# Prompt attention scores in two float32r passes with stacked query parts, and attention begun beside the third head

## The chip, the cores and the metric

The kernel runs on one core of one Trainium2 chip, in one launch. The metric is the device time of a launch in microseconds (us); smaller is better.

## The reference, cut to what matters

One layer of a hybrid decoder: a normalised input of 1024 prompt tokens and 64 sample tokens (8 sequences of 8) goes through one input projection whose columns feed a pooling mixer (256), a gated linear recurrence (HGRN2, 4 heads, 512) and a cross-attention (4 heads of 64) into 256 memory tokens. Their outputs are joined to 1024 columns and go through an output projection, then a gated feed-forward block. The change concerns the cross-attention of the prompt:

```python
def cross_attn(qx, mem_k, mem_v):
    q = qx.reshape(B, L, XATTN_HEADS, XATTN_DH).astype(jnp.float32)
    s = jnp.einsum("blhd,bmhd->bhlm", q, mem_k.astype(jnp.float32)) * (XATTN_DH ** -0.5)
    p = jax.nn.softmax(s, axis=-1)
    o = jnp.einsum("bhlm,bmhd->blhd", p, mem_v.astype(jnp.float32))
```

## The kernel before, in words

Everything lies feature by token: a tile has 128 features on the partitions and tokens along the free axis. Projections are done in float32r: each operand is split into a high part (a copy rounded to float32r, on ACT) and a low part (the rest, by a subtraction on DVE), and a product takes three matmuls, high by high, high by low and low by high (`gemm`, L282 to L284). One projection is 8 slices of the input times 3 token chunks of 362 or 364 columns.

The projections follow a list of six windows (`WIN`, L228). Letters name the columns: `q`, `i`, `f` a head's query, value and forget gate, `x` the attention's queries (two tiles `qx`, two heads of 64 features each), `g` the output gates, `u` the pooling input. Beside each window run generators: `hgrn(h)` the recurrence of a head, `xattn()` the attention, `pool_mix()` the pooling. `weave` calls the projections one after the other and takes from each generator as many steps (yields) as it is given a count for; `drain` runs a generator to its end. The order in which each engine gets its instructions follows from this, from due waits between tiles and from the free buffers, in a scheduler that sorts by priority.

In `xattn()` first the sample tokens are done: scores against the cached keys, a softmax, transposes, and eight blocks of value products into the tile `so` (L614; each block 32 small matmuls of 16 columns). Then follows the prompt, in eight blocks of 128 tokens. `scores(n)` makes four matmuls in float32, one per head: 64 features (one half of the partitions) by 128 queries and 256 memory keys (L631, into `xs`). A softmax follows on DVE and ACT. The next step transposes the probabilities on PE (`xtp`, L647), copies them on ACT (`xt`, L648), multiplies them with the memory values (`xo`, L655, 32 matmuls of 32 output columns each) and copies the result into `cat` on ACT (L658). Scores run one block ahead.

After the last window comes the output projection (`po`, L953 to L955). It needs the eight tiles of `cat` in high and low parts (`c`, L915 and the line after it) and its weights split (`ow000h`, L924, and `ow000l`, L925).

Other names in the rows: `pu` and `pg` are the projections of `u` and `g`, `oss` (L809) the sums of a head's squares, `Us` (L822) the state product of the sample tokens with 64 rows, `pp` (L555) the pooling mixer's matmul, `kv` (L478, L481) the memory projection, `whi` and `wlo` (L213, L214) the parts of the weights.

Of the kernel before, what the change touches and what calls it, by code (L numbers as in the profile page):

```python
# [10 lines left out]
F32 = mybir.dt.float32  # L11
F32R = mybir.dt.float32r
I32 = mybir.dt.int32
U8 = mybir.dt.uint8
AF = mybir.ActivationFunctionType
ALU = mybir.AluOpType
# [4 lines left out]
NP = 1024  # L21
# [6 lines left out]
RB = 34  # L28
# [22 lines left out]
def trunk(ctx, tc, I, O):  # L51
    nc = tc.nc
    const = ctx.enter_context(tc.tile_pool(name="const", bufs=1))
    rowp = ctx.enter_context(tc.tile_pool(name="rowp", bufs=1))
# [18 lines left out]
    mm = nc.tensor.matmul  # L73
    act = nc.scalar.activation
    tt = nc.vector.tensor_tensor
# [3 lines left out]
    def row(name, cols=1106, p=128):  # L79
        return rowp.tile([p, cols], F32, tag="row", name=name, bufs=RB)  # L80

    def hrow(name, cols=512, p=128, dt=F32):
        return now["wk"].tile([p, cols], dt, tag="half", name=name, bufs=HB)
# [10 lines left out]
    def bank(name, shape):  # L94
        if now["name"] == "down":
            return acc(name, shape)
        return now["psB"].tile(shape, F32, tag="b", name=name)
# [44 lines left out]
    for k in range(KT):  # L142
# [3 lines left out]
        if k % 2 == 0:  # L146
            q = slice(k * 128, k * 128 + 256)
# [71 lines left out]
    def weights(i, ahead=1):  # L219
# [8 lines left out]
    WIN = [  # L228
        [("q", 1), ("i", 1), ("f", 2)],
        [("q", 2), ("i", 2), ("f", 3)],  # L230
        [("q", 3), ("i", 3), ("x", 0), ("x", 1)],
        [("g", 0), ("g", 1)],
        [("u", 0), ("u", 1)],
        [("g", 2), ("g", 3)],
    ]
# [256 lines left out]
    mkT, mvt = memkv()  # L492
# [67 lines left out]
    def softmax(name, ps, p):  # L560
        mx, sm = tiny(f"{name}mx", 2), tiny(f"{name}sm", 2)
        nc.vector.tensor_reduce(out=mx, in_=ps, axis=AX.X, op=ALU.max)
        ts(out=mx, in0=mx, scalar1=-0.125, scalar2=None, op0=ALU.mult)
        for j in range(2):
            act(out=p[:, j, :], in_=ps[:, j, :], func=AF.Exp, bias=mx[:, j:j + 1], scale=0.125, accum_out=sm[:, j:j + 1])
        nc.vector.reciprocal(out=sm, in_=sm)
        for j in range(2):
            ts(out=p[:, j, :], in0=p[:, j, :], scalar1=sm[:, j:j + 1], scalar2=None, op0=ALU.mult)
# [6 lines left out]
    def xattn():  # L575
        qs = hrow("qs").rearrange("p (f b c) -> p f b c", f=2, b=8)
        nc.gpsimd.memset(qs, 0.0)
        for ft in range(2):
            cat[6 + ft] = row(f"cat{6 + ft}", NT)
            for half in range(2):  # L580
                P = slice(64 * half, 64 * half + 64)
                h = 2 * ft + half
                nc.gpsimd.tensor_copy(out=qs[P, ft, :, h * 8:h * 8 + 8],
                                      in_=qx[ft][P, NP:NT].rearrange("p (b l) -> p b l", b=8))
        ssc = bank("ssc", [128, 2, 256])
        svt = []
        for b in range(0, 8, 2):
            kts = [hrow(f"skt{b + i}").rearrange("p (f m) -> p f m", f=2) for i in range(2)]
            for i in range(2):
                nc.sync.dma_start(out=kts[i], in_=I["skT"][b + i])  # L590
            for ft in range(2):
                for i in range(2):
                    o = 32 * ((b + i) % 4)
                    mm(ssc[o:o + 32, b // 4, :], qs[:, ft, b + i, :], kts[i][:, ft, :], start=ft == 0, stop=ft == 1,
                       tile_position=(0, o))
            yield
        spr = hrow("spr").rearrange("p (g m) -> p g m", g=2)
        softmax("xs", ssc, spr)
        yield
        stp = bank("stp", [128, 4, 128])  # L600
        for i in range(4):
            nc.tensor.transpose(stp[:, i, :], spr[:, i // 2, (i % 2) * 128:(i % 2) * 128 + 128], ident)
        spT = hrow("spT").rearrange("p (g t c) -> p g t c", g=2, t=2)
        act(out=spT, in_=stp.rearrange("p (g t) c -> p g t c", g=2), func=AF.Copy)
        yield
        so = bank("so", [128, 2, 8, 16])
        for b in range(8):
            v_ = hrow(f"svt{b}").rearrange("p (t f) -> p t f", t=2)
            nc.sync.dma_start(out=v_, in_=I["sv"][b])
            for ft in range(2):  # L610
                for t in range(2):
                    o = 32 * (b % 4) + 16 * ft
                    for c in range(0, 128, 32):
                        mm(so[c:c + 32, ft, b, :], v_[:, t, ft * 128 + c:ft * 128 + c + 32], spT[:, b // 4, t, o:o + 16],  # L614
                           start=t == 0, stop=t == 1, tile_position=(0, c))
            yield
        for ft in range(2):
            for half in range(2):
                P = slice(64 * half, 64 * half + 64)
                act(out=cat[6 + ft][P, NP:NT].rearrange("p (b l) -> p b l", b=8),  # L620
                    in_=so[P, ft, :, half * 8:half * 8 + 8], func=AF.Copy)
        yield
        probs = {}

        def scores(n):
            pr = [hrow(f"xp{n}{hf}").rearrange("p (f m) -> p f m", f=2) for hf in range(2)]
            scs = [bank(f"xs{n}{hf}", [128, 2, 256]) for hf in range(2)]
            for ft in range(2):
                for hf in range(2):
                    P = slice(64 * hf, 64 * hf + 64)  # L630
                    mm(scs[hf][:, ft, :], qx[ft][P, n * 128:n * 128 + 128], mkT[P, ft, :], start=True, stop=True)  # L631
            for hf in range(2):
                softmax(f"x{n}{hf}", scs[hf], pr[hf])
            probs[n] = pr

        scores(0)
        for n in range(8):
            if n < 7:
                scores(n + 1)
            yield  # L640
            pr = probs.pop(n)
            ps = bank(f"xo{n}", [128, 2, 128])
            pT = [hrow(f"xt{n}{hf}").rearrange("p (f t l) -> p f t l", f=2, t=2) for hf in range(2)]
            for hf in range(2):
                tp = bank(f"xtp{n}{hf}", [128, 4, 128])
                for i in range(4):
                    nc.tensor.transpose(tp[:, i, :], pr[hf][:, i // 2, (i % 2) * 128:(i % 2) * 128 + 128], ident)  # L647
                act(out=pT[hf], in_=tp.rearrange("p (f t) l -> p f t l", f=2), func=AF.Copy)  # L648
            for ft in range(2):
                for t in range(2):  # L650
                    for hf in range(2):
                        h = 2 * ft + hf
                        for c in range(0, 64, 32):
                            o = 64 * hf + c
                            mm(ps[o:o + 32, ft, :], mvt[:, t, h * 64 + c:h * 64 + c + 32], pT[hf][:, ft, t, :],  # L655
                               start=t == 0, stop=t == 1, tile_position=(0, o))
            for ft in range(2):
                act(out=cat[6 + ft][:, n * 128:n * 128 + 128], in_=ps[:, ft, :], func=AF.Copy)  # L658
            yield
# [180 lines left out]
    def weave(units, *fillers, finish=1.0):  # L840

        done = [0] * len(fillers)
        for i, u in enumerate(units):
            for t, _ in enumerate(u()):
                part = min(1.0, (4 * i + t + 1) / (finish * 4 * len(units)))
                more = True
                while more:
                    more = False
                    for j, (g, n) in enumerate(fillers):
                        if done[j] < int(part * n + 1e-6):  # L850
                            next(g, None)
                            done[j] += 1
                            more = True
# [4 lines left out]
    def units(lst, chunk_major=False):  # L858
        if chunk_major:
            o = [(nm, j, c) for c in range(3) for nm, j in lst]  # L860
        else:
            o = [(nm, j, c) for nm, j in lst for c in range(3)]
        return [lambda nm=nm, j=j, c=c: project(nm, j, c, EV[nm](j)) for nm, j, c in o]

    hg = [hgrn(h) for h in range(4)]
    HS, XS, PS = 20, 31, 9
# [7 lines left out]
    drain(hg[1])  # L874
    head_rows(3)
    qx = [row(f"qx{j}", NT) for j in range(2)]
    weave(units(WIN[2]), (hg[2], HS))
    drain(hg[2])
    xa, pm = xattn(), pool_mix()
    weave(units(WIN[3]), (hg[3], HS), (xa, 16))  # L880
    drain(hg[3])
    nc.gpsimd.dma_start(out=O["pstate"], in_=sout)
    up, us, sbs = pool_rows()
    weave(units(WIN[4]), (xa, 10))
    weave(units(WIN[5], True), (pm, PS), (xa, 5), finish=0.7)
    drain(pm, xa)


# [709 lines left out]
    for mi in range(2):  # L1598
        for i in (0, 2):
            x = X[mi, 1, 0][:, i:i + 2]  # L1600
# [117 lines left out]
```

## Time and profile before

| what | us |
|---|---|
| median of 3 runs | 1228.74 (1227.69 to 1230.68) |
| the profiled execution | 1228.64 |
| its span | 1226.9 |

The span is the time from the first to the last instruction that the profiler shows. In a timeline each row is a run of instructions of one line: its start, the time from its first start to its last end, the line, the operation, the result and the operands, the form (rows by columns of the array that a matmul uses, then partitions by columns of the data) and how many records. Ends of matmuls are modelled and overlap; the distance from start to start tells the pace. A matmul in float32 has two records, one in float32r has one, but both are shown as f32. Stages of the program begin at about 188 us (third window, projections of `x` at 224), 259 (fourth), 312 (fifth), 351 (sixth) and 402 (output projection).

### The profile page before, as it was taken

How to read it: one execution, taken by the hardware profiler on the slowest of the kernel's cores; microseconds unless marked ns; L12 is line 12 of the kernel's file. 1: busy time of each engine (PE TensorE's matmuls, PEld its weight loads, DVE VectorE, ACT ScalarE, POOL GpSimd, SP SyncE). 2: the span in 40 equal slices, each digit the busy share in tenths (PEclk: the TensorE clock that was granted, in tenths of full speed). 3: DMA queues.
4: the chain of work that ended last, by engine and by line, in shares of the span. 5: the costliest groups of instructions: out<-in, count | busy, mean ns of one | idle time of the engine just before them, and what ended most of it. 6: DMA issues, size and time to landing. Idle time of an engine off the chain costs nothing.

```text
span 1226.9 us, 27524 instructions
## 1 busy us (share of the span) xinstructions
PE 1192.4 (97%) x11332; PEld 1148.2 (94%) x11332; DVE 925.3 (75%) x1675; ACT 545.4 (44%) x1044; POOL 260.9 (21%) x297
## 2 busy tenths in 40 slices
PE   6999999999999999899999999999999999999996
PEld 6999898978878899899999999999999999999996
DVE  7685869487877458989779878987786969868534
ACT  7743534223455455743333332333333445554542
POOL 0000000000000001445454554544323000100242
PEclk9999999999999999999999999999999999999998
DMA  8031111223102643213454354344212597345333
GB/s 270 27 121 53 37 53 53 78 79 120 39 23 91 236 135 115 89 61 132 146 191 139 107 173 159 119 157 158 89 53 70 190 333 263 90 128 151 96 97 111
DMA packets 75838, 148.20 MB, mean 121 GB/s; under 512 B 9264, under 2 KB 31280, under 8 KB 75712
## 3 DMA queue, kind: packets, MB, share of 16 engines
q1 hardware_dynamic: 71776, 140.73, 34.9%
q0 software_dynamic: 1568, 5.39, 1.2%
q8 instruction: 89, 1.46, 0.5%
q10 hardware_dynamic: 2368, 0.32, 0.2%
q14 instruction: 37, 0.30, 0.1%
HBM read 110.48 MB, written 35.93 MB: 119 GB/s over the span
## 4 chain that ended last, share of the span: by engine, by line
PE 59%; DVE 8%; issue 3%; ACT 1%; POOL 0%; DVEq 0%; ACTq 0%; POOLq 0%
PE po L955 2%; PE po L953 2%; PE po L954 2%; PE uUa L1232 2%; PE pV L1381 2%; PE pV L1382 2%; PE pV L1383 2%; PE uUa L1230 2%; PE pP L1381 2%; PE pP L1382 2%; PE uUa L1231 2%; PE uPa L1232 2%; PE pP L1383 2%; PE pU L1381 2%; PE uPa L1230 2%
## 5 line engine op out<-in xcount | busy, mean ns | idle before, releaser
L1369 DVE TENSOR_TENSOR dlp<-drp,dhp 128x512 fp32r<-128x512 f32 x77 | 54.2, 712 | 35.3 <-ACT dhp L1368 34.3
L1368 ACT ACTIVATE dhp<-drp 128x512 fp32r<-128x512 f32 x77 | 47.7, 626 | 69.8 <-PE pU L1382 21.2
L1348 DVE TENSOR_TENSOR xop<-B,xop 128x544 fp32r<-128x544 f32 x70 | 50.0, 729 | 11.6 <-ACT xop L1374 11.6
L1374 ACT ACTIVATE xop<-B 128x544 fp32r<-128x544 f32 x70 | 43.9, 648 | 25.1 <-DVE xop L1348 13.0
L1381 PE MATMUL pU<-xop,dhp 128*128 128x272 f32 x176 | 50.8, 288 | 0.1
L1382 PE MATMUL pU<-xop,dhp 128*128 128x272 f32 x176 | 50.7, 288 | 0.0
L1382 PE MATMUL pV<-xop,dhp 128*128 128x272 f32 x176 | 50.7, 288 | 0.0
L1381 PE MATMUL pV<-xop,dhp 128*128 128x272 f32 x176 | 50.6, 288 | 0.0
L1383 PE MATMUL pV<-xop,dlp 128*128 128x272 f32 x176 | 50.6, 287 | 0.0
L1383 PE MATMUL pU<-xop,dlp 128*128 128x272 f32 x176 | 50.5, 287 | 0.0
L1193 DVE TENSOR_TENSOR g<-g,uc 128x272 f32<-128x272 f32 x66 | 46.1, 699 | 0.8
L1263 ACT ACTIVATE g<-g 128x1104 f32<-128x1104 f32 x22 | 24.8, 1128 | 40.8 <-DVE g L1262 40.8
L1260 DVE SCALAR_TENSOR_TENSOR g<-a,vec,g 128x1104 f32<-128x1104 f32 x22 | 31.8, 1444 | 14.5 <-ACT g L1258 14.5
L1166 POOL TENSOR_TENSOR us0a<-ura 128x512 f32<-128x512 f32 x11 | 18.9, 1718 | 106.3 <-DVE ow160l L925 86.5
L1381 PE MATMUL pP<-xop,dhp 128*128 128x272 f32 x144 | 41.4, 288 | 0.0
L1382 PE MATMUL pP<-xop,dhp 128*128 128x272 f32 x144 | 41.4, 288 | 0.0
L1383 PE MATMUL pP<-xop,dlp 128*128 128x272 f32 x144 | 41.4, 287 | 0.0
L1262 DVE SCALAR_TENSOR_TENSOR g<-a,vec,g 128x1104 f32<-128x1104 f32 x22 | 39.6, 1802 | 0.0
L1266 DVE TENSOR_TENSOR g<-g,ra 128x560 f32<-128x560 f32 x22 | 36.9, 1676 | 0.0
L824 POOL DMA_DIRECT2D out_sstate<-s x8 | 4.3, 541 | 139.9 <-DVE s L823 139.9
L1381 PEld LDWEIGHTS pU<-xop,dhp 128*128 128x128 f32 x176 | 33.1, 188 | 0.3 <-DVE xd L1500 0.3
L1383 PEld LDWEIGHTS pU<-xop,dlp 128*128 128x128 f32 x176 | 33.2, 188 | 0.0
(2313 smaller groups left out, 5053.5 us busy)
## 6 DMA issues: line engine op xcount, KB each, us to landing
ds<-in_wdown SPq DMA_DIRECT2D x44, 256.0 KB, 3.1
ura<-in_wup SPq DMA_DIRECT2D x22, 512.0 KB, 4.4
urb<-in_wup SPq DMA_DIRECT2D x22, 512.0 KB, 3.5
sd<-ds SPq DMA_DIRECT2D x44, 256.0 KB, 2.0
drp<-sd SPq DMA_DIRECT2D x44, 256.0 KB, 2.8
fd<-g SPq DMA_DIRECT2D x20, 544.0 KB, 3.9
B<-fd SPq DMA_DIRECT2D x40, 272.0 KB, 5.6
drp<-in_wdown SPq DMA_DIRECT2D x33, 256.0 KB, 3.2
```

The source lines that it names most:

```text
L1193: tt(out=dst, in0=dst, in1=s_, op=ALU.mult)
L1230: mm(ps, wh[:, w], xh[:, k], start=first and k == 0, stop=False, skip_group_check=True)
L1232: mm(ps, wl[:, w], xh[:, k], start=False, stop=k == 3, skip_group_check=True)
L1262: stt(out=cw[:, 0:1104], in0=aw[:, 0:1104], scalar=col(V_CW, 3 * f), in1=cw[:, 0:1104], op0=ALU.mult, op1=ALU.add)
L1266: tt(out=tail, in0=tail, in1=ra[0], op=ALU.mult)
L1348: tt(out=out, in0=in0, in1=in1, op=ALU.subtract)
L1368: act(out=wh, in_=raw, func=AF.Copy)
L1369: tt(out=wl, in0=raw, in1=wh.bitcast(F32), op=ALU.subtract)
L1374: act(out=t[:, 0], in_=x, func=AF.Copy)
L1381: mm(ps, w[0][:, c], h, start=start, stop=False, skip_group_check=True)
L1382: mm(ps, w[0][:, c], l, start=False, stop=False, skip_group_check=True)
L1383: mm(ps, w[1][:, c], h, start=False, stop=stop, skip_group_check=True)
```

## The change

The third window does its two `x` projections first. `xattn()` is begun beside the second half of that window, with 8 of its steps, where before it began with the fourth window; in the windows behind it there are 16, 9 and 1 step in place of 16, 10 and 5, and it has three steps more. After the sample attention it makes `KS` (the high part of the memory keys, held on both halves of the partitions), `KL` (their low part) and four tiles `QS` (for each head the high part of its queries on one half of the partitions and the low part on the other). The copies within a half are done by ACT and DVE; the way to the other half is a DMA on SP, two for `KS` and four for `QS`. Each matmul of `scores(n)` is replaced by two in float32r: one with all 128 rows (high and low queries times `KS`, which adds both products), and one with 64 rows (high queries times `KL`), which adds to it.

```diff
--- before.py
+++ after.py
@@ -228,7 +228,7 @@
     WIN = [
         [("q", 1), ("i", 1), ("f", 2)],
         [("q", 2), ("i", 2), ("f", 3)],
-        [("q", 3), ("i", 3), ("x", 0), ("x", 1)],
+        [("x", 0), ("x", 1), ("q", 3), ("i", 3)],
         [("g", 0), ("g", 1)],
         [("u", 0), ("u", 1)],
         [("g", 2), ("g", 3)],
@@ -620,6 +620,26 @@
                 act(out=cat[6 + ft][P, NP:NT].rearrange("p (b l) -> p b l", b=8),
                     in_=so[P, ft, :, half * 8:half * 8 + 8], func=AF.Copy)
         yield
+
+        KS = rowp.tile([128, 2, 2, 256], F32R, tag="row", name="KS", bufs=RB)
+        KL = hrow("KL", dt=F32R).rearrange("p (f m) -> p f m", f=2)
+        QS = {}
+        for hf in range(2):
+            P, o = slice(64 * hf, 64 * hf + 64), slice(64 - 64 * hf, 128 - 64 * hf)
+            act(out=KS[P, :, hf, :], in_=mkT[P], func=AF.Copy)
+            tt(out=KL[P], in0=mkT[P], in1=KS[P, :, hf, :].bitcast(F32), op=ALU.subtract)
+            nc.sync.dma_start(out=KS.bitcast(F32)[o, :, hf, :], in_=KS.bitcast(F32)[P, :, hf, :])
+        yield
+        for ft in range(2):
+            for hf in range(2):
+                P, o = slice(64 * hf, 64 * hf + 64), slice(64 - 64 * hf, 128 - 64 * hf)
+                t = rowp.tile([128, 1024], F32R, tag="row", name=f"QS{ft}{hf}", bufs=RB)
+                act(out=t[P], in_=qx[ft][P, 0:NP], func=AF.Copy)
+                lo = qx[ft].bitcast(F32R)[P, 0:NP]
+                tt(out=lo, in0=qx[ft][P, 0:NP], in1=t[P].bitcast(F32), op=ALU.subtract)
+                nc.sync.dma_start(out=t.bitcast(F32)[o], in_=lo.bitcast(F32))
+                QS[ft, hf] = t
+            yield
         probs = {}
 
         def scores(n):
@@ -628,7 +648,9 @@
             for ft in range(2):
                 for hf in range(2):
                     P = slice(64 * hf, 64 * hf + 64)
-                    mm(scs[hf][:, ft, :], qx[ft][P, n * 128:n * 128 + 128], mkT[P, ft, :], start=True, stop=True)
+                    q = QS[ft, hf][:, n * 128:n * 128 + 128]
+                    mm(scs[hf][:, ft, :], q, KS[:, ft, hf, :], start=True, stop=False)
+                    mm(scs[hf][:, ft, :], q[P], KL[P, ft, :], start=False, stop=True)
             for hf in range(2):
                 softmax(f"x{n}{hf}", scs[hf], pr[hf])
             probs[n] = pr
@@ -874,15 +896,16 @@
     drain(hg[1])
     head_rows(3)
     qx = [row(f"qx{j}", NT) for j in range(2)]
-    weave(units(WIN[2]), (hg[2], HS))
+    xa, pm = xattn(), pool_mix()
+    weave(units(WIN[2][:2]), (hg[2], HS // 2))
+    weave(units(WIN[2][2:]), (hg[2], HS - HS // 2), (xa, 8))
     drain(hg[2])
-    xa, pm = xattn(), pool_mix()
     weave(units(WIN[3]), (hg[3], HS), (xa, 16))
     drain(hg[3])
     nc.gpsimd.dma_start(out=O["pstate"], in_=sout)
     up, us, sbs = pool_rows()
-    weave(units(WIN[4]), (xa, 10))
-    weave(units(WIN[5], True), (pm, PS), (xa, 5), finish=0.7)
+    weave(units(WIN[4]), (xa, 9))
+    weave(units(WIN[5], True), (pm, PS), (xa, 1), finish=0.7)
     drain(pm, xa)
```

The lines behind L620 stand 20 to 23 lines lower in the changed kernel.

PE, the first two blocks of scores (`xs00` and `xs01` are block 0, `xs10` block 1; `Us` is a state product, `pu` and the `L28x` lines projections). Before:

```order
L822 MATMUL Us30_4119<-Vs30_4116,Ks3_3864 128x512
L822 MATMUL Us31_4126<-Vs31_4123,Ks3_3864 128x512
L631 MATMUL xs00_4132<-mkv_945,qx0_2446 128x256
L631 MATMUL xs01_4133<-mkv_945,qx0_2446 128x256
L631 MATMUL xs00_4132<-mkv_945,qx1_2447 128x256
L631 MATMUL xs01_4133<-mkv_945,qx1_2447 128x256
L631 MATMUL xs10_4158<-mkv_945,qx0_2446 128x256
L631 MATMUL xs10_4158<-mkv_945,qx1_2447 128x256
L631 MATMUL xs11_4159<-mkv_945,qx0_2446 128x256
L631 MATMUL xs11_4159<-mkv_945,qx1_2447 128x256
L282 MATMUL pu01_4255<-h2h_175,whi20_3758 128x362
```

And with the change:

```order
L813 MATMUL o30_3971<-Q3_2444,S30_3899 128x128
L652 MATMUL xs00_3982<-KS_3867,QS00_3904 128x256
L653 MATMUL xs00_3982<-KL_3868,QS00_3904 128x256
L652 MATMUL xs01_3983<-KS_3867,QS01_3908 128x256
L653 MATMUL xs01_3983<-KL_3868,QS01_3908 128x256
L652 MATMUL xs00_3982<-KS_3867,QS10_3925 128x256
L653 MATMUL xs00_3982<-KL_3868,QS10_3925 128x256
L652 MATMUL xs01_3983<-KS_3867,QS11_3929 128x256
L653 MATMUL xs01_3983<-KL_3868,QS11_3929 128x256
L652 MATMUL xs10_4012<-KS_3867,QS00_3904 128x256
L653 MATMUL xs10_4012<-KL_3868,QS00_3904 128x256
L652 MATMUL xs10_4012<-KS_3867,QS10_3925 128x256
```

Eight matmuls on 64 rows have become runs that change between 128 rows (L652) and 64 rows (L653) at each step; the other matmuls of block 1 follow some rows later in the same manner.

PE, among the products of the sample attention (`so`; `U`, `ktps`, `o` and `dg` belong to the last head). Before:

```order
L763 MATMUL U31_3845<-Vt3_3340,Kt31_3808 128x128 x4
L777 MATMUL ktps3_3862<-cst_123,K3_1704 64x128
L789 MATMUL o30_3871<-scT_952,Vt3_3340 128x128 x2
L614 MATMUL so_3699<-spT_3650,svt2_3784 32x16 x16
L791 MATMUL o30_3871<-Q3_2444,S30_3779 128x128
L614 MATMUL so_3699<-spT_3650,svt3_3815 32x16 x16
L789 MATMUL o30_3871<-scT_952,Vt3_3340 128x128
L791 MATMUL o30_3871<-Q3_2444,S30_3779 128x128
```

And with the change, where projections stand before and behind:

```order
L284 MATMUL pg00_3354<-h3h_179,wlo18_3111 128x364
L699 MATMUL dg3_3373<-Q3_2444,K3_1704 32x32 x32
L699 MATMUL dgs3_3407<-Q3_2444,K3_1704 32x32 x2
L614 MATMUL so_3264<-spT_3222,svt2_3412 32x16 x16
L282 MATMUL pg00_3354<-h4h_183,whi18_3110 128x364
L283 MATMUL pg00_3354<-h4l_184,whi18_3110 128x364
L284 MATMUL pg00_3354<-h4h_183,wlo18_3111 128x364
```

The blocks of `so` stand earlier, one by one between projections, where before seven of the eight stood within 28 rows, among matmuls of the last head.

ACT, from the last block of attention to the output projection's weights (`sg` is a gate's sigmoid). Before:

```order
L648 ACTIVATE xt70_4941<-xtp70_4943 128x512
L648 ACTIVATE xt71_4942<-xtp71_4949 128x512
L915 ACTIVATE c20_5076<-o0_1491 128x544
L915 ACTIVATE c30_5079<-o1_2234 128x544
L658 ACTIVATE cat6_3319<-xo7_4940 128x128
L658 ACTIVATE cat7_3322<-xo7_4940 128x128
L915 ACTIVATE c40_5082<-o2_3029 128x544
L915 ACTIVATE c50_5085<-o3_3866 128x544
L915 ACTIVATE c60_5088<-cat6_3319 128x544
L915 ACTIVATE c70_5091<-cat7_3322 128x544
L915 ACTIVATE c00_5094<-cat0_4701 128x544
L834 ACTIVATE sg22_4992<-gz22_4991 128x362
```

With the change:

```order
L856 ACTIVATE sg22_5048<-gz22_5047 128x362
L856 ACTIVATE sg32_5079<-gz32_5078 128x362
L556 ACTIVATE cat1_4916<-pp10_4968,vec_78 128x364
L556 ACTIVATE cat1_4916<-pp11_4971,vec_78 128x362
L556 ACTIVATE cat1_4916<-pp12_4974,vec_78 128x362
L670 ACTIVATE xt70_4997<-xtp70_4999 128x512
L670 ACTIVATE xt71_4998<-xtp71_5005 128x512
L680 ACTIVATE cat6_2955<-xo7_4996 128x128
L680 ACTIVATE cat7_2958<-xo7_4996 128x128
L938 ACTIVATE c20_5132<-o0_1491 128x544
L938 ACTIVATE c30_5135<-o1_2234 128x544
L938 ACTIVATE c40_5138<-o2_3059 128x544
L938 ACTIVATE c50_5141<-o3_3966 128x544
L947 ACTIVATE ow000h_5110<-or00_5106 128x512
```

The last block's copies (`xt70`, `xt71`, `cat6`, `cat7`) have moved behind the last gate's sigmoid `sg32` and the pooling copies, and the first `c` copies behind them.

## Rows read from the trace of the kernel before

**Rows 1.** The page of the profile, part 1: busy time of each engine
```profile
PE 1192.4 (97%) x11332; PEld 1148.2 (94%) x11332; DVE 925.3 (75%) x1675; ACT 545.4 (44%) x1044; POOL 260.9 (21%) x297
```

**Rows 2.** Table by stage: stretch, us, busy PE PEld DVE ACT POOL, PEclk, DMA
```profile
223.70:311.60 87.90, 86.20 (x1292) 76.09 (x1291) 57.88 (x125) 27.41 (x58) 4.56 (x10) 0.98 0.32 97
311.60:351.40 39.80, 39.48 (x275) 33.70 (x274) 34.33 (x85) 17.28 (x51) 2.87 (x4) 1.00 0.10 29
351.40:401.60 50.20, 48.30 (x422) 39.46 (x420) 37.76 (x86) 28.83 (x81) 2.95 (x6) 1.00 0.24 73
```

**Rows 3.** Line L631, the scores: records, ns min/median/max, first and last start
```profile
L631 PEld LDWEIGHTS xs<-mkv,qx x64: 182/186/187, 319.4 to 374.4; 64*128 64x128 f32 x64
L631 PE MATMUL xs<-mkv,qx x64: 376/376/481, 319.4 to 374.6; 64*128 64x256 f32 x64
```

**Rows 4.** Timeline of PE round the scores: start, us, line, out<-in, tile form
```profile
319.43 0.48 PE L631 MATMUL xs<-mkv,qx 64*128 64x256 f32 x1
...
322.03 1.13 PE L631 MATMUL xs<-mkv,qx 64*128 64x256 f32 x4 [0.22 <-DVE s L823]
323.08 0.44 PE L282 MATMUL pu<-h2h,whi 128*128 128x362 f32 x1
...
338.90 0.70 PE L631 MATMUL xs<-mkv,qx 64*128 64x256 f32 x2
339.53 1.07 PE L655 MATMUL xo<-xt,mkv 128*32 128x128 f32 x28
340.53 1.13 PE L631 MATMUL xs<-mkv,qx 64*128 64x256 f32 x6
341.58 0.88 PE L647 MATMUL xtp<-cst,xp 128*128 128x128 f32 x6
```

**Rows 5.** Timeline of PE, memory projection: float32r, 256 columns
```profile
70.48 0.40 PE L478 MATMUL kv<-mh,whi 128*128 128x256 f32 x2
70.72 0.41 PE L481 MATMUL kv<-whi,mh 128*128 128x256 f32 x2
```

**Rows 6.** Timeline of PE, a change from 128 to 64 rows and back
```profile
256.83 0.32 PE L284 MATMUL px<-h7h,wlo 128*128 128x362 f32 x1
257.09 1.98 PE L822 MATMUL Us<-Vs,Ks 64*128 64x512 f32 x4
259.00 0.43 PE L282 MATMUL pg<-h0h,whi 128*128 128x364 f32 x1
259.27 0.33 PE L283 MATMUL pg<-h0l,whi 128*128 128x364 f32 x1
259.44 0.33 PE L284 MATMUL pg<-h0h,wlo 128*128 128x364 f32 x1
```

**Rows 7.** Timeline of PE, the sample attention's products (L614)
```profile
307.02 0.27 PE L614 MATMUL so<-spT,svt 128*32 128x16 f32 x10 [1.69 <-issue]
```

**Rows 8.** Table by stretch, behind that stall; PEclk is the granted clock
```profile
307.80:311.30 3.50, 3.50 (x42) 3.08 (x42) 2.14 (x5) 1.78 (x6) 0.00 (x0) 0.51 0.22 22
```

**Rows 9.** Timeline of PE, last gate projection to first output matmul
```profile
399.35 0.33 PE L284 MATMUL pg<-h7h,wlo 128*128 128x362 f32 x1
401.58 0.40 PE L953 MATMUL po<-c,ow000h 128*128 128x272 f32 x1 [1.90 <-DVE sg L835]
```

**Rows 10.** By tile or line: copies on ACT, wait of L655, subtraction on DVE
```profile
L648 ACT ACTIVATE xt<-xtp x16: 592/607/624, 337.6 to 391.1; 128x512 f32<-128x512 f32 x16
...
  ACT xt L648: 1.8, 7
...
L915 ACT ACTIVATE c<-o x8: 642/646/662, 391.6 to 435.0; 128x544 fp32r<-128x544 f32 x8
...
L658 ACT ACTIVATE cat<-xo x16: 271/274/278, 340.6 to 393.2; 128x128 f32<-128x128 f32 x16
...
L214 DVE TENSOR_TENSOR wlo<-raw,whi x24: 683/1225/1254, 8.7 to 352.8; 128x1024 fp32r<-128x1024 f32 x22, 128x512 fp32r<-128x512 f32 x2
```

**Rows 11.** The page of the profile, part 6: a DMA of 256 KB
```profile
sd<-ds SPq DMA_DIRECT2D x44, 256.0 KB, 2.0
```

## The prediction

> **What bounds the kernel now.** I read the page's busy shares first: TensorE (PE) is busy 1192.4 of 1226.9 us, DVE 75% and ACT 44% [rows 1]. So a change counts by what it does to PE's queue. Next comes the table by stage [rows 2]: in the two stages that carry prompt attention, 311.6 to 351.4 and 351.4 to 401.6 us, PE is busy 39.48 of 39.80 and 48.30 of 50.20 us, with DVE at 34.33 and 37.76. PE sets the pace there, and DVE has room, though not much. Then I go to the line that the diff touches, the score matmuls [rows 3], to their neighbours in time [rows 4], to a float32r matmul of the same 256 columns [rows 5], and to the places where PE changes between matmuls of 64 and of 128 rows [rows 4, 6].
>
> **Term 1, the scores.** Before, 32 float32 matmuls show as 64 records [rows 3]. A lone matmul between two other kinds takes 338.90 to 339.53, 0.63 us for two records; a group of three takes 340.53 to 341.58, 1.05 us, less than three times as much, because the two halves of the rows overlap somewhat [rows 4]. One block of 128 tokens has one of each, so 1.68; six blocks make 10.1. The first two blocks lie between 319.43 and 323.08, 3.65 us together with a bit of a state product [rows 4]; I take 3.4. Sum 13.5 us.
> Now there are 64 matmuls, 32 of 128 rows and 32 of 64 rows, in strict alternation. The float32r matmuls of 256 columns run one per 0.12 us (70.48 to 70.72 for two) [rows 5]. Streaming alone is 64 x 0.12 = 7.7 us, which would save 5.8.
> But PE changes its row shape 64 times, where before all scores were of one shape. What does such a change cost? At 257.09 four 64-row matmuls begin, and at 259.00 comes the next 128-row matmul. That one is followed after 0.27 us (259.00 to 259.27), while its successor is followed after 0.17 (259.27 to 259.44): 0.10 us more behind the change [rows 6]. Ahead of it, the last 128-row matmul before the 64-row group is followed after 0.26 us (256.83 to 257.09), against the same pace of 0.17: 0.09 more [rows 6]. The score groups agree: four records take 322.03 to 323.08, 1.05 us, and two take 0.63 [rows 4], so two more records cost 0.42, one 0.21, and a group has 0.63 - 0.42 = 0.21 on top of its records, for its way in and its way out. So a change of shape costs 0.09 + 0.10 = 0.19 us. The 64 matmuls then take 64 x (0.12 + 0.19) = 19.8 us. Against them stand the 13.5 and some 0.5 that seven of the old groups cost the matmul after them (by rows 6 up to 0.10 each): **+5.8 us**.
> Bounds: no cost of a change gives -5.8. If a whole weight load (0.187 us [rows 3]) came out at each change, with some 0.09 beside it, it would be 64 x 0.40 - 14.0 = +11.6. I take 0.19, since it is nearest to the very change of shape in rows 6.
> The Trainium skill, "TensorEngine Tiling (Array Packing)", Tiling Modes, says that going from one tiling mode to another drains the engine; it gives no price. Read as a drain only, this would be the 0.09 ahead of the change, and the scores would come to 64 x 0.21 - 14.0 = -0.6 us instead of +5.8. The rows show a further 0.10 behind the change, and the measurement decides.
>
> **Term 2, the sample attention.** Its `so` matmuls (L614) now stand among projections, a block at a time, where before most of them stood together with other small matmuls behind the last projections of their stage. There PE stood 1.69 us for nothing that the profile shows [rows 7], and from 307.8 to 311.3 its granted clock was 0.51 [rows 8], the 1.2 GHz level; half speed for 3.5 us loses 1.7. If the small matmuls are spread, the stall goes, and the drop that came right behind it has no reason that I see: **-3.4 us**. Bounds: 0 (both only move) and -3.4.
>
> **Term 3, from attention to the output projection.** The last block's transposes, value products and copies now come after the last gate projection (`pg`), where before some 40 matmuls of projections stood behind them. On ACT, four `c` copies and the first weight copy `ow000h` now stand behind the copies of that block. Before, PE went from 399.35 to 401.58, 2.06 us beyond the 0.17 of a projection [rows 9]. After the last `pg` (0.2) there now are: three float32 pool matmuls of 362 columns, six records (0.21 for 256 columns, so 0.30 each: 1.8); eight transposes (six take 0.88 us, the last one's 0.27 included [rows 4], 0.11 each: 0.9); about 1.0 until ACT has made its second copy (0.607 each [rows 10]); 32 value products (28 take 339.53 to 340.53 [rows 4]: 1.15, with their end 1.4); two copies of 0.274 and four of 0.646, of which some 0.1 overlaps [rows 10]: 2.75; and `ow000h`, like the 0.607 of the same size: 0.6. Sum 8.65 us, of which PE works 0.2 + 1.8 + 0.9 + 1.15 = 4.05. Idle 4.6 in place of 2.1: **+2.5 us**. Bounds: 0, if other work takes the place, to +4.2, if PE's clock is low there for another stretch that loses 1.7.
>
> **Term 4, small waits.** Before, the value products wait for ACT's copies seven times, 1.8 us together [rows 10]. Blocks four to seven are now squeezed into the last projection stage, each with only two or three projections between transposes and products: two or three waits more at 0.3 to 0.5 each, some 1.0. The last head's K and Q chains stand on DVE behind new subtractions: one such subtraction at most, some 0.5 of it not covered. I take **+1.5**, with bounds 0 and 3.
>
> **At no cost.** Four ACT copies of 64x1024 and two of 64x512 (two and one times the 0.607 of 512 columns [rows 10]) are 6.1 us; four subtractions on DVE (1.225 for 1024 columns [rows 10]) and two of half that are 6.1. They fall into the stages from 223.7 to 311.6, where ACT is busy 27.41 and DVE 57.88 of 87.90 us [rows 2]. Without that room each would add up to 6. Six DMAs of 128 and 256 KB are issued on SP (2.0 us for 256 KB [rows 11]). They wait there for the subtractions, and two weight loads stand behind them; their data is needed only in the last projection stage, 40 us later. Moving the two `x` projections ahead of `q` and `i` keeps every projection.
>
> **Sum.** 5.8 - 3.4 + 2.5 + 1.5 = +6.4 us. The profiled execution took 1228.64 us (span 1226.9), level with the median of 1228.74: **1235.0 us**. A measurement of this kernel can tell about 0.3%, 3.7 us, from no change.
>
> **Rivals.**
> 1. A change of row shape costs nothing between two matmuls that add to the same sums. Then the scores give -5.8 and the sum is -5.2: 1223.4, faster. For it: no row has this very pair, 128 and 64 rows of float32r. Against it: rows 4 and 6 show a price in both directions. It decides below some 0.02 us per change. Chance 0.12.
> 2. Only the drain is paid (0.09): the scores give -0.6 and the sum is 0: 1228.6, no difference. The weights of the next shape would have to load during the drain; rows 6 speak against it. Chance 0.13.
> 3. Prices as above, but the way to the output projection does not grow and the small waits are covered by the longer scores: 5.8 - 3.4 = +2.4: 1231, within the bound. Chance 0.13.
> 4. The stall and the clock drop only move, since there are as many small matmuls as before: 6.4 + 3.4: 1238.4, slower. Chance 0.15.
> 5. The two passes run at float32's pace of two records each, so that the change does not do what it says: 64 x (0.42 + 0.19) - 14 = +25 for the scores: 1254. Rows 5 show float32r as one record of 0.12. Chance 0.02.
>
> **How the numbers follow.** The forecast as it stands has 0.45; it and rivals 4 and 5 are slower by over 0.3%: 0.62. Rivals 2 and 3 lie within: 0.26. Rival 1: 0.12. The range leaves out rivals 1 and 5 and takes in the rest: from 1227, a little below rival 2, to 1241, the sum with the higher bound of the weight load.
>
> **What would show it.** Right: the two score lines have 32 records each, one follows the other after about 0.31 us, and a block takes some 2.5 us in place of 1.68; no wait for "issue" in the `so` group; full clock from 304 to 312; the first `po` some 8.6 us after the last `pg`. Wrong: score matmuls that follow at 0.12 us (rival 1) or 0.21 (rival 2); 2 us of idle time or less ahead of `po` (rival 3); a stall among small matmuls that turns up elsewhere (rival 4).

## The result, and the profile after

The changed kernel takes 1236.95 us (median of five runs, 1235.6 to 1242.53) against 1228.74 before; the ratio is 1.0077, 95% interval 1.0063 to 1.0091. It is slower, by 8.2 us between the medians. The profiled execution took 1235.6 us with a span of 1233.8, 6.9 more than before. Its mean granted clock is 0.995; the other four runs have 0.993 to 0.989, and the one at 0.989 is the one of 1242.53 us. So 6.9 us is what the traces can explain, and a part of the rest is the clock.

The page of the changed kernel, busy time by engine, and below it the table by stage (stretch, its us, busy PE, PEld, DVE, ACT, POOL, then PEclk and DMA):

```profile
PE 1199.5 (97%) x11332; PEld 1150.6 (93%) x11332; DVE 932.5 (76%) x1681; ACT 550.7 (45%) x1050; POOL 258.0 (21%) x297
```

```profile
304.70:351.00 46.30, 46.30 (x369) 39.51 (x369) 35.30 (x89) 19.87 (x57) 1.35 (x5) 1.00 0.11 32
351.00:409.40 58.40, 54.41 (x434) 42.95 (x432) 42.52 (x97) 27.57 (x79) 3.86 (x8) 1.00 0.26 87
```

PE is busy 7.1 us longer than in [rows 1]. The stages that carry the prompt's attention have shifted (the fifth window now begins at 304.7 and the first output matmul comes at 409.4): in the first PE is busy throughout, in the second it is idle for 4.0 of 58.4 us, where in [rows 2] it was idle for 1.9 of 50.2.

The two score lines of the changed kernel (records, ns min/median/max, first and last start, form):

```profile
L652 PE MATMUL xs<-KS,QS x32: 279/384/555, 307.5 to 383.2; 128*128 128x256 f32 x32
```
```profile
L653 PE MATMUL xs<-KL,QS x32: 378/381/383, 307.8 to 383.5; 64*128 64x256 f32 x32
```

32 records of 128 rows and 32 of 64, in place of the 64 in [rows 3]. Their timeline on PE, from block 0:

```profile
307.76 0.38 PE L653 MATMUL xs<-KL,QS 64*128 64x256 f32 x1
308.07 0.39 PE L652 MATMUL xs<-KS,QS 128*128 128x256 f32 x1
308.39 0.38 PE L653 MATMUL xs<-KL,QS 64*128 64x256 f32 x1
...
310.90 0.38 PE L653 MATMUL xs<-KL,QS 64*128 64x256 f32 x1
311.21 0.44 PE L283 MATMUL pu<-h0l,whi 128*128 128x364 f32 x1
311.48 0.33 PE L284 MATMUL pu<-h0h,wlo 128*128 128x364 f32 x1
```

One follows the other after 0.31 to 0.32 us (307.76, 308.07, 308.39), where two float32r matmuls of this size without a change of shape in [rows 5] follow after 0.12. Three of the 64 are different, each the first of a group: 0.29 (307.47), 0.21 (312.32) and 0.49 (335.76). Behind the last one (310.90) comes a projection after 0.31, and the projection itself is followed after 0.27 (311.48) where [rows 6] has 0.17 between its like. Added up from start to next start, the score matmuls take 20.05 us; those of before take 13.50 when added up in the same way.

Where the price lies is seen best at 312.32. That matmul of 128 rows stands behind a projection of 128 rows, so only one change touches it, the one behind it, and it takes 0.21 us (312.32 to 312.52), not 0.31:

```profile
312.32 0.28 PE L652 MATMUL xs<-KS,QS 128*128 128x256 f32 x1
312.52 0.38 PE L653 MATMUL xs<-KL,QS 64*128 64x256 f32 x1
```

The other 0.10 shows on the weight loads (PEld). Behind a change the load starts with its own matmul, at 308.07 in the block above. The second line is a load of the variant in which the shape never changes (**No change of shape**, further down); its matmul starts at 321.23, 0.11 us behind the load:

```profile
308.07 0.19 PEld L652 LDWEIGHTS xs<-KS,QS 128*128 128x128 f32 x1
```
```profile
321.12 0.19 PEld L653 LDWEIGHTS xs<-KS,QS 128*128 128x128 f32 x1
```

The stretch after the last gate projection, on PE:

```profile
400.62 0.33 PE L284 MATMUL pg<-h7h,wlo 128*128 128x362 f32 x1
401.36 2.07 PE L555 MATMUL pp<-pr,poolw 128*128 128x364 f32 x6 [0.41 <-DVE pr L548]
403.27 1.03 PE L669 MATMUL xtp<-cst,xp 128*128 128x128 f32 x8
404.57 1.55 PE L677 MATMUL xo<-xt,mkv 128*32 128x128 f32 x32 [0.27 <-ACT xt L670]
409.36 0.59 PE L976 MATMUL po<-c,ow000h 128*128 128x272 f32 x1 [3.24 <-ACT ow000h L947]
```

From 400.62 to 409.36 are 8.74 us, where [rows 9] has 2.23. And the clock (table by stretch):

```profile
303.00:312.00 9.00, 9.00 (x56) 7.29 (x56) 7.38 (x19) 4.72 (x12) 0.65 (x2) 1.00 0.40 142
409.10:412.50 3.40, 3.14 (x13) 2.97 (x14) 3.40 (x7) 3.40 (x7) 0.00 (x0) 0.50 0.10 18
```

The stretch from 303 to 312 us is at full clock, where [rows 8] has 0.51; the first half-speed stretch of the changed kernel behind the start of the program begins at 409.1, with the output projection, where the kernel before had its second.

### The profile page after: what moved, and what is told of

It is laid out like the page before. It is cut to its first block, busy times and chain, and to the rows that moved or that the text cites. A ratio compares the mean times of both kernels' runs of the same rounds, so it can differ in the third digit from the quotient of the medians.

```text
span 1233.8 us, 27543 instructions
## 1 busy us (share of the span) xinstructions
PE 1199.5 (97%) x11332; PEld 1150.6 (93%) x11332; DVE 932.5 (76%) x1681; ACT 550.7 (45%) x1050; POOL 258.0 (21%) x297
## 4 chain that ended last, share of the span: by engine, by line
PE 82%; DVE 9%; ACT 3%; issue 3%; DMA 2%; SPq 0%; DVEq 0%; POOL 0%; ACTq 0%; POOLq 0%
PE po L976 2%; PE po L978 2%; PE po L977 2%; PE uUa L1255 2%; PE pV L1404 2%; PE uPa L1255 2%; PE pV L1405 2%; PE pV L1406 2%; PE pP L1405 2%; PE pP L1404 2%; PE uUa L1253 2%; PE pP L1406 2%; PE uUa L1254 2%; PE pU L1404 2%; PE uPa L1253 2%
## 5 line engine op out<-in xcount | busy, mean ns | idle before, releaser
L1371 DVE TENSOR_TENSOR xop<-B,xop 128x544 fp32r<-128x544 f32 x70 | 49.9, 729 | 11.4 <-ACT xop L1397 11.3
L213 ACT ACTIVATE whi<-raw 128x1024 fp32r<-128x1024 f32 (+1 forms) x24 | 24.6, 1023 | 22.9 <-PE px L283 5.5
L214 DVE TENSOR_TENSOR wlo<-raw,whi 128x1024 fp32r<-128x1024 f32 (+1 forms) x24 | 28.3, 1180 | 6.9 <-ACT whi L213 6.6
```

Source lines behind the costliest of these rows:

```text
L1371: tt(out=out, in0=in0, in1=in1, op=ALU.subtract)
```

## The experiments

Two theories stood against each other. A: the loss lies in the score matmuls themselves, 0.19 us for each change of row shape, plus a longer way to the output projection. B: the loss comes from the new order of the work, and the scores cost what they cost before. A third, C, came up for the way to the output projection. All diffs are against the changed kernel.

**Old scores in the new order.** The part of `xattn` that makes `KS`, `KL` and `QS` is left out, with bare steps in its place:

```diff
-                    q = QS[ft, hf][:, n * 128:n * 128 + 128]
-                    mm(scs[hf][:, ft, :], q, KS[:, ft, hf, :], start=True, stop=False)
-                    mm(scs[hf][:, ft, :], q[P], KL[P, ft, :], start=False, stop=True)
+                    mm(scs[hf][:, ft, :], qx[ft][P, n * 128:n * 128 + 128], mkT[P, ft, :], start=True, stop=True)
```

> The new order of the attention, with the float32 scores of before and without KS, KL and QS (three bare steps stand in their place). Theory A (the loss lies in the new score matmuls, 0.19 us at each change of row shape, and in the longer way that their preparation gives the last block): scores back at 13.5 us, the stall of 1.7 us and its clock drop gone, the last value products ahead of the last gate projections again as before: 1225 to 1228 us, under the kernel before. Theory B (the loss comes from the new order, whatever the scores are): 1235 to 1238 us.

Measured: 1228.28 us, ratio to the kernel before 0.9997 (0.9988 to 1.0007). The loss is gone with the new scores and their preparation, so B falls; the variant with 128 rows, below, keeps the preparation and tells the two apart. But there is no gain either: the median is 0.3 us above A's range. The profiled execution shows where the gain went; it is the slowest of the ten, 1229.59 us at a mean granted clock of 0.993, and the four at 0.995 took 1226.67 to 1227.43. Scores 12.1 us; no wait for "issue" among the `so` matmuls, which take 3.04 us in place of 5.00; but the sample's score products (`ssc`) take 5.58 in place of 3.95, and a wait of 1.22 us stands ahead of the last head's `o`. So PE reaches the output projection only 1.0 us earlier than before (400.56 against 401.58). Then it loses that again:

```profile
398.54 0.33 PE L284 MATMUL pg<-h7h,wlo 128*128 128x362 f32 x1
400.56 0.40 PE L958 MATMUL po<-c,ow000h 128*128 128x272 f32 x1 [1.69 <-DVE sg L839]
...
402.36 0.60 PE L960 MATMUL po<-c,ow000l 128*128 128x272 f32 x1 [1.15 <-DVE ow000l L930]
```

```profile
401.50:408.30 6.80, 5.95 (x26) 5.95 (x27) 2.44 (x5) 1.26 (x2) 0.00 (x0) 0.50 0.77 280
```

The half-speed stretch that was at 307.8 us is gone, but the one at the output projection is now 6.8 us long instead of 3.4. So in this execution the new order by itself takes one clock drop away in one place and gets it back in another.

**New scores in the old order.** `WIN[2]`, the place where `xattn()` is created and the steps of the windows as before (19, 10 and 5 steps).

> The new scores in the order of before (attention begun with the fourth window, x projected last, 19, 10 and 5 steps). Theory A: scores 20 us, 6.5 more than before, and an even longer way to the output projection, since two blocks' value products now stand behind the last gate projections' start: 1237 to 1242 us. Theory B: 1228 to 1231 us.

Measured: 1246.86 us, ratio 1.0155 (1.0130 to 1.0180), 5 us beyond the top of what A expected. Between the last gate projection and the output there are now two blocks of attention and one half of the pooling mixer, with waits on DVE and ACT between them:

```profile
405.04 0.32 PE L284 MATMUL pg<-h7h,wlo 128*128 128x362 f32 x1
407.93 2.41 PE L677 MATMUL xo<-xt,mkv 128*32 128x128 f32 x32 [2.57 <-ACT xt L670]
413.19 4.00 PE L555 MATMUL pp<-pr,poolw 128*128 128x364 f32 x6 [2.84 <-DVE pr L548]
...
418.71 1.55 PE L677 MATMUL xo<-xt,mkv 128*32 128x128 f32 x32 [0.31 <-ACT xt L670]
424.60 0.59 PE L975 MATMUL po<-c,ow000h 128*128 128x272 f32 x1 [4.33 <-ACT ow000h L946]
```

```profile
339.30:349.50 10.20, 10.20 (x31) 8.83 (x31) 3.24 (x9) 1.77 (x5) 0.00 (x0) 0.50 0.06 24
407.50:417.70 10.20, 6.92 (x42) 4.35 (x43) 5.57 (x12) 2.92 (x7) 0.56 (x1) 0.50 0.31 125
```

The waits in brackets are 2.57, 2.84, 0.31 and 4.33, 10.0 us together; and twice PE has half its clock for 10.2 us, of which the first stretch, fully busy, loses 5.1. A had the scores and the direction, but not these clock drops. The trace is that of the slowest of the four executions, 1251.24 us at a mean granted clock of 0.984; the two at 0.990 and 0.991 took 1244.73 and 1245.05, so part of these drops belongs to this execution. The earlier start of the attention is therefore worth much to the new scores (1246.86 against 1236.95 us), though nothing to the old ones.

**Pairs.** Two score matmuls of 128 rows, then two of 64 rows:

```diff
             for ft in range(2):
                 for hf in range(2):
+                    mm(scs[hf][:, ft, :], QS[ft, hf][:, n * 128:n * 128 + 128], KS[:, ft, hf, :], start=True, stop=False)
+                for hf in range(2):
                     P = slice(64 * hf, 64 * hf + 64)
-                    q = QS[ft, hf][:, n * 128:n * 128 + 128]
-                    mm(scs[hf][:, ft, :], q, KS[:, ft, hf, :], start=True, stop=False)
-                    mm(scs[hf][:, ft, :], q[P], KL[P, ft, :], start=False, stop=True)
+                    mm(scs[hf][:, ft, :], QS[ft, hf][P, n * 128:n * 128 + 128], KL[P, ft, :], start=False, stop=True)
```

> The changed kernel with the score matmuls in pairs: two of 128 rows, then two of 64 rows, so at most half as many changes of row shape. Theory A: 24 to 32 changes fewer at 0.19 us, 4.5 to 6 us less than the changed kernel: 1231 to 1233 us, scores at 14 to 15.5 us. Theory B, or a price that belongs to each 64-row matmul and not to the change: no difference, 1236 to 1238 us.

Measured: 1233.33 us, ratio 1.0040 (1.0025 to 1.0055). Block 2 on PE:

```profile
320.94 0.51 PE L650 MATMUL xs<-KS,QS 128*128 128x256 f32 x2
321.37 0.39 PE L653 MATMUL xs<-KL,QS 64*128 64x256 f32 x2
321.69 0.51 PE L650 MATMUL xs<-KS,QS 128*128 128x256 f32 x2
```

Four matmuls take 320.94 to 321.69, 0.75 us, in place of 4 x 0.31 = 1.24. Two rows hold the two 64-row matmuls: they take 0.32 us together (321.37 to 321.69), as much as one alone did. Their halves run beside each other; in the trace the second begins 0.003 us after the first. All scores together take 13.46 us, 6.6 less than 20.05, for the same 64 matmuls. (That is more than A expected, and the time is 0.3 us above its range: PE then waits over 2 us for the pooling sums, as in the next run.) Of the 0.49 us saved on four matmuls, 0.38 are the two changes that are gone and some 0.1 is the second 64-row matmul, which runs beside the first. So the pairs alone could still be read as a price of each 64-row pass. What speaks against it are the 128-row matmuls: the first of the pair at 321.69 is followed by the second at 321.91 (the row holds both), after 0.22 us and not 0.12, though no 64-row matmul starts between them, so the time belongs to the change.

**No change of shape.** `KL` is held on both halves, as `KS` is, and the second matmul has 128 rows:

```diff
-        KL = hrow("KL", dt=F32R).rearrange("p (f m) -> p f m", f=2)
+        KL = rowp.tile([128, 2, 2, 256], F32R, tag="row", name="KL", bufs=RB)
...
-            tt(out=KL[P], in0=mkT[P], in1=KS[P, :, hf, :].bitcast(F32), op=ALU.subtract)
+            tt(out=KL[P, :, hf, :], in0=mkT[P], in1=KS[P, :, hf, :].bitcast(F32), op=ALU.subtract)
...
+            nc.sync.dma_start(out=KL.bitcast(F32)[o, :, hf, :], in_=KL.bitcast(F32)[P, :, hf, :])
...
-                    mm(scs[hf][:, ft, :], q[P], KL[P, ft, :], start=False, stop=True)
+                    mm(scs[hf][:, ft, :], q, KL[:, ft, hf, :], start=False, stop=True)
```

> The changed kernel with KL held on both halves as KS is (two more DMAs), so that the second matmul has 128 rows too and the row shape never changes; it adds low by low. Theory A: 64 matmuls at 0.12 us, some 8 us for the scores, 12 less than the changed kernel, the way to the output projection as long as there: 1224 to 1226 us. Theory B: 1236 to 1238 us.

Measured: 1229.77 us, ratio 1.0016 (1.0007 to 1.0026), 7 us under the changed kernel, but 4 above the top of what A expected. Block 2 and the way to the output on PE:

```profile
320.89 0.38 PE L653 MATMUL xs<-KS,QS 128*128 128x256 f32 x1
321.11 0.28 PE L654 MATMUL xs<-KL,QS 128*128 128x256 f32 x1
321.23 0.28 PE L653 MATMUL xs<-KS,QS 128*128 128x256 f32 x1
```

```profile
389.34 0.33 PE L284 MATMUL pg<-h7h,wlo 128*128 128x362 f32 x1
391.98 3.22 PE L555 MATMUL pp<-pr,poolw 128*128 128x364 f32 x6 [2.31 <-DVE pr L548]
395.00 1.61 PE L670 MATMUL xtp<-cst,xp 128*128 128x128 f32 x8
...
401.60 0.39 PE L977 MATMUL po<-c,ow000h 128*128 128x272 f32 x1 [3.24 <-ACT ow000h L948]
```

The matmuls follow after 0.12 us, the first of this block after 0.22: it stands behind small matmuls of 32 columns, which are another form too, and its weight load starts with it (both at 320.89). All scores take 9.33 us, 10.7 less, and the last gate projection is 11.3 us earlier (389.34 against 400.62). The first output matmul is only 7.8 us earlier: PE now waits 2.31 us for the pooling sums on DVE, where the changed kernel waited 0.41, and the granted clock is 0.51 from 392.7 to 396.1 (three pool matmuls take 3.02 us instead of 1.91). What PE saved had been the cover for DVE.

**Preparation first.** The making of `KS`, `KL` and `QS` ahead of the sample attention, once with the scores as changed, once with 128 rows throughout, and in a third run, in place of that move, the scores and their softmax at the scheduler's high priority. All three bring the last block's value products ahead of the last gate projections in PE's order.

> The changed kernel with the making of KS, KL and QS moved ahead of the sample attention; the scores alternate between 128 and 64 rows as there. In the order of PE the last block's value products then stand some 40 projections ahead of the output projection again. Theory A (scores +6.5, way to the output projection +2.5): the 4 to 5 us of idle time ahead of the first output matmul go back to about 2, scores stay at 20 us: 1233 to 1235 us. Theory C (that way is set by DVE and ACT, which are late wherever the preparation stands): the idle time only moves: 1236 to 1238 us.

> Both edits together: the second score matmul with 128 rows too, and the preparation ahead of the sample attention. Theory A: the scores at 9.3 us, and the 8 us of idle time between the last gate projection and the first output matmul that the first edit alone left go down to 2 or 3: 1223 to 1226 us, under the kernel before. Theory C: 1228 to 1231 us.

> The second score matmul with 128 rows, the preparation where the change has it, and the scores with their softmax at high priority for the scheduler, which moves the last block ahead of the last gate projections by another way. Theory A: 1223 to 1227 us. Theory C: 1228 to 1231 us.

Measured: 1237.96 us, ratio 1.0075 (1.0060 to 1.0091), for the first; 1225.99 us, ratio 0.9973 (0.9964 to 0.9983), for the second; 1228.76 us, ratio 1.0009 (0.9999 to 1.0019), for the third. The first shows no gain over the changed kernel, and A's range was missed by 3 us. The way to the output on PE, and DVE beside it:

```profile
405.33 0.33 PE L284 MATMUL pg<-h7h,wlo 128*128 128x362 f32 x1
407.66 0.39 PE L976 MATMUL po<-c,ow000h 128*128 128x272 f32 x1 [2.00 <-DVE c L939]
...
410.53 0.59 PE L978 MATMUL po<-c,ow000l 128*128 128x272 f32 x1 [2.23 <-DVE ow000l L948]
```

```profile
409.79 0.68 DVE L948 TENSOR_TENSOR ow000l<-or,ow000h 128x512 fp32r<-128x512 f32 x1
```

The wait ahead of the first output matmul is down to 2.00 us from 3.24. But a second one, of 2.23, stands behind it: the low part of the weights, `ow000l`, is made on DVE (409.79) behind the last low parts of `c`. Both together are 4.2 us, and the changed kernel has 3.9 in its three waits. So C holds for this place: DVE and ACT have to make eight pairs of `c` and the weights there, and moving the last block of attention ahead of the last gate projections does not shorten that. On ACT the first `c` copy still stands behind that block's copies:

```profile
400.87 0.66 ACT L938 ACTIVATE c<-o 128x544 fp32r<-128x544 f32 x1
```

It starts 4.5 us ahead of the last gate projection (405.33); before, the first one started 7.8 us ahead (391.6 in [rows 10], 399.35 in [rows 9]). Over the five kernels whose last block stands ahead, the two waits together grow as this lead shrinks: 2.5 us at a lead of 7.8 (before), 2.8 at 6.0 (old scores in the new order), 4.2 at 4.5 (this run), 4.7 at 4.1 and 6.0 at 2.0 (the second and the third run). No run moved the `c` copies alone, so that this lead is the cause is not shown. The half-speed stretches, 3.4 us at 309.7 and 6.8 us at 408.6 where the changed kernel has 3.4 up to that place, cost up to 3.4 us more; and the stall of [rows 7] is back among the sample's small matmuls (waits for "issue" of 1.28 us at 276.72 and 0.86 at 280.55).

The second run is the fastest of all. The same place on PE:

```profile
393.23 0.33 PE L284 MATMUL pg<-h7h,wlo 128*128 128x362 f32 x1
395.85 0.39 PE L977 MATMUL po<-c,ow000h 128*128 128x272 f32 x1 [2.29 <-DVE sg L858]
...
398.92 0.60 PE L979 MATMUL po<-c,ow000l 128*128 128x272 f32 x1 [2.43 <-DVE ow000l L949]
```

The two waits are still there, 2.29 and 2.43 us. What it gains on the kernel before is ahead of them: PE reaches the last gate projection 6.1 us earlier (393.23 against 399.35), with scores of 9.8 us. The sample attention is not all gain; its stall is still there, at another place:

```profile
276.39 0.44 PE L634 MATMUL so<-spT,svt 128*32 128x16 f32 x32 [1.51 <-issue]
```

A's range of 1223 to 1226 was met at its edge, in part by another path than A gave. The waits on the way to the output are 4.7 us, more than the 2.5 of before, and only 1.2 less than the 5.9 that the run with 128 rows alone has there (2.31, 3.24 and 0.34). Beside that this run has one half-speed stretch fewer than that one and spends 1.6 us less on `ssc` (3.94 against 5.58). The third run, 1.8 us above A's range, shows the same limit (waits of 3.92 and 2.03 us).

**The fastest version in the old order.**

> The fastest version so far (second score matmul with 128 rows, preparation ahead of the sample attention) with the order of before: attention begun with the fourth window, x projected last, 19, 10 and 5 steps. In PE's order two blocks' value products then stand behind the last gate projection. Theory A (the new scores need the earlier start, since the work on DVE and ACT that they add makes the blocks late): scores at 9 to 10 us again, but 8 to 11 us of idle time ahead of the first output matmul, so 5 to 9 us more than that version: 1231 to 1236 us. Theory B (the earlier start is worth nothing): 1225 to 1228 us.

Measured: 1233.85 us, ratio 1.0055 (1.0038 to 1.0072), 7.9 us more than in the new order. Scores 9.51 us, and on PE:

```profile
389.22 2.41 PE L678 MATMUL xo<-xt,mkv 128*32 128x128 f32 x32 [2.38 <-ACT xt L671]
395.02 4.00 PE L555 MATMUL pp<-pr,poolw 128*128 128x364 f32 x6 [3.40 <-DVE pr L548]
400.34 1.56 PE L678 MATMUL xo<-xt,mkv 128*32 128x128 f32 x32 [0.25 <-ACT xt L671]
406.23 0.59 PE L976 MATMUL po<-c,ow000h 128*128 128x272 f32 x1 [4.33 <-ACT ow000h L947]
```

Waits of 2.38, 3.40, 0.25 and 4.33 us, 10.4 together, and half the clock from 389.0 to 399.3. The earlier start is what lets the new scores pay.

## Why the prediction was right

The direction and the size came out: 1235.0 was forecast, 1236.95 measured, from a sum of +6.4 where the traces differ by 6.9. The first term agrees for the reason that was given; that the whole sum agrees to 0.5 us is in part luck, since terms 3 and 4 were too high together by about as much as was left out.

- **Term 1, the scores, +5.8.** Measured +6.55 (20.05 against 13.50). The price of a change of shape, 0.19 us from [rows 6], is the step that carried the forecast; 0.31 per matmul was expected and 0.31 to 0.32 is there in all but three places. The three variants of the same 64 matmuls confirm it: 20.05 us with 64 changes, 13.46 with pairs, 9.33 with none. (20.05 - 9.33) / 64 is 0.17 per change; it comes out a little under 0.19 because 1.65 of the 9.33 are prices at the ends of the groups (64 x 0.12 is 7.68); (20.05 - 7.68) / 64 is 0.19. One of the forecast's supports is weaker than it was put: the score groups of [rows 4] do not agree on 0.21 per record and per group, since a group of six records takes the same 1.05 us as one of four. In it the two halves run beside each other, as in the pairs. The price rests on [rows 6]. Rivals 1 and 2 fall: no score matmul beside a change follows after 0.12, and the 0.21 of rival 2 is there only at 312.32. The Trainium skill's rule in "TensorEngine Tiling (Array Packing)", Tiling Modes, that a change of mode drains the engine, agrees with the trace as far as it goes, with the 0.09 ahead of a change; the 0.10 behind it is not in that rule.
- **Term 2, the sample attention, -3.4.** The `so` matmuls take 3.04 us instead of 5.00, and the half-speed stretch behind them is gone: 1.96 + 1.7 = 3.7. Rival 4 falls for this kernel. The runs add a warning: in the variant with old scores the clock drop came back at the output projection, and in the one with the preparation first at 309.7 us; the stall itself came back in both variants with the preparation first (1.28 and 1.51 us) and in the last one (0.96). Neither gain is safe.
- **Term 3, the way to the output, +2.5.** 8.65 us were worked out from the last gate projection to the first output matmul, and 8.74 are there. So close an agreement is luck: PE works 4.8 of them and not 4.05, and is idle for 3.9 and not 4.6. (One item is added up wrongly too: two copies of 0.274 and four of 0.646 less 0.1 are 3.0, not 2.75; the trace has 2.52 for the six, from 406.17 to 408.69.) PE's waits are 0.41, 0.27 and 3.24, 3.9 together. Before there were 1.90 and, three matmuls later, 0.64 for the weights' low part, which is gone now: 3.9 - 2.5 = +1.4. So the term was about 1 us too high, since the second wait of before was left out of it. Of its two reasons, the block behind the last gate projection is not what makes the waits: with the block moved ahead they are 4.2. The other, the `c` copies behind the block's copies on ACT, remains in that run, and may be the cause.
- **Term 4, small waits, +1.5.** A wait of about the 0.5 that was put down for the last head's Q chain is there, ahead of the window that carries the prompt's scores:

```profile
291.95 0.22 PE L699 MATMUL sc<-Q,K 128*32 128x16 f32 x5 [0.44 <-DVE Q L770]
```

Right ahead of Q on DVE stand a weight's split and a gate (289.53, 290.67), and the new subtraction further ahead (286.16), so its part in the wait is not shown. The 1.0 for the value products did not come: in the stages from 304.7 to the last gate projection PE is idle for less than 0.1 us. It was built on a misreading. The seven waits of 1.8 us in [rows 10] are those of the weight loads (PEld), which run ahead of the matmuls; PE itself waited for none of these copies in the kernel before. Its waits from 319 to 399 us are the first line below; the second is that of the weight loads (us in total, times, the longest):

```profile
PE xs L631 <- DVE s L823: 0.2, 1, 0.2
```
```profile
PEld xo L655 <- ACT xt L648: 1.8, 7, 0.4
```

In place of these waits there is a price that was not in the sum: the sample's score products (`ssc`, L594) are now scattered between projections and take 5.58 us in place of 3.95, from start to next start. They have another form than the projections, so a change at each way in and out, as in term 1, is the likely reason; no run tests it. That is +1.6, and that it made up for the waits is luck. With these, 6.55 - 3.7 + 1.4 + 0.4 + 1.6 = 6.3; the last 0.6 us is spread over lines that each differ by less than 1.
- **At no cost.** ACT and DVE hid the preparation in the order chosen here, but for at most the 0.44 us above. In the old order there are 10.0 us of waits on the way to the output; how much of them is the preparation's work no run tells.

So rival 3 is half true, and hidden by an omission of about the same size. What is not settled: why a half-speed stretch at the output projection is 3.4 us long in one kernel and 6.8 in another. There it begins in or right behind a wait of PE. Two others do not: the ones at 339.3 us (new scores in the old order) and at 309.7 (preparation first) begin with no wait that the timeline shows in the 25 us before them; what stands right ahead is a long group of alternating score matmuls, from 335.97 and from 304.02. The changed kernel has such a group at 307.47 and keeps its full clock, so the group is not shown to be the cause.

## What to carry to other kernels

Count how often an engine changes its form, not only how much it streams: here scores that should have taken 6 us less took 6.5 more, because each matmul of 64 rows stood between two of 128, and the price could be read in the trace of before where the two meet. Doing two small ones beside each other took 6.6 of it away, bringing the small operand to the full height 10.7. When the busiest engine gets faster, look for what it covered: 11 us saved in the scores gave 7 at the end, since DVE and ACT were next on the way to the output projection.

## What the runs showed of the hardware

- A matmul of 256 columns in float32r costs 0.12 us among its like and 0.31 between matmuls of the other row shape, at 128 as at 64 rows: 0.09 ahead of a change (0.21 at 312.32, which has only that) and 0.10 behind one, where the weight load starts together with its matmul (308.07) and not 0.11 ahead of it (321.12).
- Two 64-row matmuls on the two halves of the array, into different tiles of sums, cost 0.32 us together between matmuls of 128 rows, as much as one: they start 0.003 us apart.
- The granted clock falls to its lower level (0.50 to 0.51) for 3.4 to 10.2 us at a time, mostly in or right behind a wait of PE, twice with none in the timeline for 25 us before. Between 20 and 430 us the changed kernel and the fastest version spend 3.4 us at that level, the kernel before 6.8, and the profiled execution of the new scores in the old order 27. Half of such a time is lost where PE is busy throughout, which is as much as some of the edits are worth.
